# Twelve weight tiles held back instead of eight in the last block of an output product, and the last row tile's layer norm on VectorE alone

## The chip, the cores and the metric

The kernel runs on one core of a Trainium2 chip. Its metric is the device time of one execution in microseconds, the median of three runs. The engines spoken of here are TensorE (PE in the profile, its weight loads PEld), VectorE (DVE), ScalarE (ACT), GpSimd (POOL) and SyncE (SP), which issues most of the transfers between the chip's memory (HBM) and the on-chip memory SBUF. TensorE writes its sums into PSUM.

## What is computed

One layer of a decoder trunk on an input of 512 rows and 2048 columns, in float32. Three attention branches are gated, summed to y, multiplied by an output matrix of 2048 x 2048, added to the scaled input and normalised row by row:

```python
y = (jax.nn.sigmoid(p["gate_fox"]) * br_fox + jax.nn.sigmoid(p["gate_swa"]) * br_swa
     + jax.nn.sigmoid(p["gate_moba"]) * br_moba)
out = jnp.einsum('bsd,de->bse', y, w_out)
return layer_norm(DEEPNORM_ALPHA * x + out, ln_g, ln_b)

def layer_norm(x, g, b):
    xf = x.astype(jnp.float32)
    mu = jnp.mean(xf, axis=-1, keepdims=True)
    var = jnp.mean(jnp.square(xf - mu), axis=-1, keepdims=True)
    return ((xf - mu) * lax.rsqrt(var + LN_EPS) * g + b).astype(x.dtype)
```

The change touches only the last product and the norm.

## The kernel before

Every float32 operand of a matmul is split into a high part, rounded to TensorE's format, and a low part, the remainder; a product is then three matmuls (high x high, low x high, high x low). ScalarE makes the high part of a weight tile (L145), VectorE the low part (L148).

**The output product.** It is tiled into four column blocks `ec` of 512 columns, four row tiles `st` of 128 rows and sixteen k tiles of 128. The weights come as tiles of 128 x 512, two of them in one load of 512 KB; a load goes to one of four buffers `raw`, and it is issued by SyncE once both tiles of the load four places earlier have been split. `prepare(i + 2)` splits a tile two steps ahead of its use. In the first three column blocks a step uses one weight tile for all four row tiles, and after the sixteenth step `residual` (L944, L945) adds the scaled input to each row tile's sum and takes the statistics of that block with `bn_stats`.

**The last column block.** Its row tile 3 is computed in two halves of 256 columns with sums of their own, so that a step has nine matmuls of 512 columns and six of 256. The first eight weight tiles are used as they come. The last eight are split into tiles of their own, `wh0` to `wh7` and `wl0` to `wl7`, which stay in SBUF (`held`); their steps in `out_step` return at once. After the loop over all steps, the held tiles are used row tile by row tile: 24 matmuls finish row tile 0, 24 row tile 1, 24 row tile 2, then 24 each of half the width finish the two halves of row tile 3. Behind each of the row tiles 0 to 2 its `residual` and its `norm` are written; the residual of the first half of row tile 3 (`residual_half`, L1043 and L1044) stands in the middle of the norm of row tile 2, that of the second half and `norm(3)` stand at the end.

**The norm of a row tile.** VectorE combines the statistics (L971), ScalarE takes the square root (L972), VectorE the reciprocal (L983) and the shift -mean/deviation (L984, one column). The 2048 columns are then shared in pieces of 512. The columns below `cut` belong to VectorE: L976 subtracts the mean and multiplies by the gain, L979 multiplies by the reciprocal and adds the bias. In the columns from `cut` on, ScalarE normalises (L987) and GpSimd multiplies by the gain (L988) and adds the bias (L989). `cut` is 1024 for the row tiles 0 to 2 and 1536 for row tile 3. SyncE stores the pieces (L998, L1002, L1006, L1007).

**Memory.** `open_last` runs after the fourth step of the first column block. It opens the pool `last`, which holds the four row tiles `z0` to `z3` with the input (loaded by GpSimd's queue, L919), gain and bias (L923), and the held weight tiles. The pool `ozy`, which held the attention branches' outputs, stays open until the end of the kernel.

Each engine works through its instructions in the order in which they are written here; no scheduler moves them.

Of the kernel before, what the change touches and what calls it, by code (L numbers as in the profile page):

```python
# [9 lines left out]
F32R = mybir.dt.float32r  # L10
# [3 lines left out]
P = 128  # L14
S = 512
D = 2048
# [71 lines left out]
def hybrid_kernel(ctx: ExitStack, tc: tile.TileContext, a: dict, out: bass.AP):  # L88
    nc = tc.nc
# [19 lines left out]
    def acc_tile(name):  # L109
        return psum.tile([P, S], F32, tag="acc", name=name, bufs=3)  # L110
# [10 lines left out]
    raws, parts = {}, {}  # L121
    held = {}
    tasks = {}

    def at(i, order, f, *args):
        tasks.setdefault(i, []).append((order, len(tasks.get(i, ())), f, args))
# [369 lines left out]
            at((m - 56) // 2, 3, f, len(GROUPS) - 1, *args)  # L496


    att_ctx = ExitStack()
    ozy = work = const = vfox = vswa = sinkc = nsink = tri = causal = band = vld = None  # L500

    def open_attention():
        nonlocal ozy, work, const, vfox, vswa, sinkc, nsink, tri, causal, band, vld
        gate_ctx.close()
        ozy = ctx.enter_context(tc.tile_pool(name="ozy", bufs=12))
        work = att_ctx.enter_context(tc.tile_pool(name="work", bufs=2))
        const = att_ctx.enter_context(tc.tile_pool(name="const", bufs=1))
        const.tile([P, 32], F32, name="room")
        vfox = const.tile([P, 4, NH, P], F32R, tag="v", name="vfox")
        vswa = const.tile([P, 4, 2, P], F32R, name="vswa")  # L510
        sinkc = const.tile([P, NH], F32, name="sinkc")
        nsink = const.tile([P, NH], F32, name="nsink")
        vld = [work.tile([P, 4, NV], F32, tag="pth", name=f"vld{j}") for j in range(2)]
        for j in range(2):
            nc.sync.dma_start(vld[j], a["vs"][j])
        nc.gpsimd.dma_start(sinkc, a["sinks"].to_broadcast([P, NH]))
        ones = work.tile([P, S], F32, tag="L", name="ones", bufs=3)
        nc.gpsimd.memset(ones, 8.0)
        tri = work.tile([P, S], F32R, tag="L", name="tri", bufs=3)
        nc.gpsimd.affine_select(tri, ones, pattern=[[1, S]], compare_op=ALU.is_ge, fill=0.0, base=0,  # L520
                                channel_multiplier=-1)
        causal = const.tile([P, P], F32, name="causal")
        nc.gpsimd.memset(causal, 0.0)
        nc.gpsimd.affine_select(causal, causal, pattern=[[-1, P]], compare_op=ALU.is_ge, fill=8 * NEG, base=0,
                                channel_multiplier=1)
        band = const.tile([P, 256], F32, name="band")
        nc.gpsimd.iota(band, pattern=[[1, 256]], base=-P, channel_multiplier=-1,
                       allow_small_or_imprecise_dtypes=True)
        nc.gpsimd.affine_select(band, band, pattern=[[-1, 256]], compare_op=ALU.is_ge, fill=NEG, base=P,
                                channel_multiplier=1)  # L530
        nc.gpsimd.affine_select(band, band, pattern=[[1, 256]], compare_op=ALU.is_ge, fill=NEG, base=-1,
                                channel_multiplier=-1)
# [205 lines left out]
    where = {}  # L738
# [66 lines left out]
    for p in range(4):  # L805
        q, k, z = [], [], []
# [10 lines left out]
    for p in range(4):  # L817
        q, z = [], []
# [16 lines left out]
    for p in range(4):  # L835
        q, k, z = [], [], []
# [76 lines left out]

    def open_last():
        mix_ctx.close()
        last = box["last"] = ctx.enter_context(tc.tile_pool(name="last", bufs=1))
        for st in range(4):
            zr.append(last.tile([P, D], F32, name=f"z{st}"))
            nc.gpsimd.dma_start(zr[st], a["xn"][st])  # L919
            stats.append(last.tile([P, 5 if st == 3 else 4, 6], F32, name=f"stats{st}"))  # L920
        for n in ("ln_gain", "ln_bias"):
            box[n] = last.tile([P, D], F32, name=n)
            nc.gpsimd.dma_start(box[n], a[n].to_broadcast([P, D]))  # L923
        box["eps"] = last.tile([P, 1], F32, name="epst")
        nc.vector.memset(box["eps"], LN_EPS)
        for n in range(8):
            held[where["o", 3] + 8 + n] = tuple(last.tile([P, S], F32R, name=f"w{x}{n}") for x in "hl")

    oacc = {}

    def out_mm(st, k, hi, lo, half=None):

        sl = slice(st * P, (st + 1) * P)
        o = oacc[st]
        if half is not None:
            cs = slice(half * 256, (half + 1) * 256)
            o, hi, lo = oacc[3 + half][:, :256], hi[:, cs], lo[:, cs]
        nc.tensor.matmul(o, yb["h"][:, k, sl], hi, start=(k == 0), stop=False)  # L938
        nc.tensor.matmul(o, yb["l"][:, k, sl], hi, start=False, stop=False)  # L939
        nc.tensor.matmul(o, yb["h"][:, k, sl], lo, start=False, stop=(k == KD - 1))  # L940
# [6 lines left out]
    def out_step(i):  # L947
        _, ec, k = ids[i]
        if k == 0:
            for st in range(4):  # L950
                oacc[st] = (acc_tile if st == 3 else att_tile)("o")
            if ec == 3:
                oacc[4] = acc_tile("o")
        if ec == 3 and k >= 8:
            return
        hi, lo = parts.pop(i)
        for st in range(3 if ec == 3 else 4):
            out_mm(st, k, hi, lo)
        if ec == 3:
            out_mm(3, k, hi, lo, 0)  # L960
            out_mm(3, k, hi, lo, 1)
        if k == KD - 1:
            for st in range(4):
                at(i, 9, residual, ec, st, oacc[st])

    def norm(st, middle=None):

        last = st == 3
        cut = 1536 if last else 1024
        mv = box["last"].tile([P, 5], F32, tag="mv", name="mv", bufs=2)  # L970
        nc.vector.bn_aggr(mv[:, 0:2], stats[st].rearrange("p a b -> p (a b)"))  # L971
        nc.scalar.activation(mv[:, 2:3], mv[:, 1:2], AF.Sqrt, bias=box["eps"])  # L972
        g, b, z, rows = box["ln_gain"], box["ln_bias"], zr[st], out[st * P:(st + 1) * P]

        def first(cs):
            nc.vector.scalar_tensor_tensor(z[:, cs], z[:, cs], mv[:, 0:1], g[:, cs], op0=ALU.subtract, op1=ALU.mult)  # L976

        def second(cs):
            nc.vector.scalar_tensor_tensor(z[:, cs], z[:, cs], mv[:, 3:4], b[:, cs], op0=ALU.mult, op1=ALU.add)  # L979

        left = [slice(c, c + S) for c in range(0, cut, S)]
        first(left[0])
        nc.vector.reciprocal(mv[:, 3:4], mv[:, 2:3])  # L983
        nc.vector.scalar_tensor_tensor(mv[:, 4:5], mv[:, 0:1], -1.0, mv[:, 3:4], op0=ALU.mult, op1=ALU.mult)  # L984
        for c in range(cut, D, S):
            cs = slice(c, c + S)
            nc.scalar.activation(z[:, cs], z[:, cs], AF.Identity, bias=mv[:, 4:5], scale=mv[:, 3:4])  # L987
            nc.gpsimd.tensor_tensor(out=z[:, cs], in0=z[:, cs], in1=g[:, cs], op=ALU.mult)  # L988
            nc.gpsimd.tensor_tensor(out=z[:, cs], in0=z[:, cs], in1=b[:, cs], op=ALU.add)  # L989
        for cs in left[1:]:  # L990
            first(cs)
        if middle:
            second(left[0])
            middle()
            left = left[1:]
            for cs in left:
                second(cs)
            nc.sync.dma_start(rows[:, :cut], z[:, :cut])  # L998
        else:
            for cs in left[:2]:  # L1000
                second(cs)
            nc.sync.dma_start(rows[:, :2 * S], z[:, :2 * S])  # L1002
            for cs in left[2:]:
                second(cs)
        if last:
            nc.sync.dma_start(rows[:, 2 * S:cut], z[:, 2 * S:cut])  # L1006
        nc.sync.dma_start(rows[:, cut:], z[:, cut:])  # L1007


    at(2, 9, open_attention)  # L1010
    dests = ([("fox", 0, 5, 0)], [("fox", 5, 3, 0), ("swa", 0, 2, 192)])
    for st in range(4):
# [19 lines left out]
    for i in range(len(ids)):  # L1032
# [4 lines left out]
        step[ids[i][0]](i)  # L1037
        for _, _, f, args in sorted(tasks.pop(i, ()), key=lambda x: x[:2]):
            f(*args)
    first = where["o", 3] + 8  # L1040
    def residual_half(c):
        z = zr[3][:, 3 * S + c * 256:3 * S + (c + 1) * 256]
        nc.vector.scalar_tensor_tensor(z, z, ALPHA, oacc[3 + c][:, :256], op0=ALU.mult, op1=ALU.add)  # L1043
        nc.vector.bn_stats(stats[3][:, 3 + c], z)  # L1044

    for st in range(3):
        for n in range(8):
            out_mm(st, 8 + n, *parts[first + n])
        if st == 2:
            for c in range(2):  # L1050
                for n in range(8):
                    out_mm(3, 8 + n, *parts[first + n], c)
        residual(3, st, oacc[st])
        norm(st, (lambda: residual_half(0)) if st == 2 else None)
    residual_half(1)
# [68 lines left out]
```

## Time and profile before

| | |
|---|---|
| median of three runs | 1357.22 us (1357.11 to 1358.02) |
| the profiled execution | 1355.71 us |
| its span, first to last instruction | 1354.0 us |
| TensorE busy | 1325.5 us, 98% |
| VectorE busy | 910.1 us, 67% |
| ScalarE busy | 650.6 us, 48% |
| GpSimd busy | 192.0 us, 14% |
| moved by DMA | 174.43 MB, 129 GB/s in the mean |

Times in the rows are microseconds from the start of the span. Matmuls are pipelined: a matmul's own length overlaps the next one's, so the distance between two starts tells the pace. The busy time of GpSimd is rough.

### The profile page before, as it was taken

The numbers are of one execution on the slowest core, as the hardware profiler recorded it, in microseconds if no ns is written. First come the engines' busy times: TensorE is split into PE (matmuls) and PEld (weight loads), VectorE is DVE, ScalarE is ACT, GpSimd is POOL, SyncE is SP. The second block draws the span as 40 slices with busy tenths as digits, with TensorE's granted clock in tenths as the row PEclk, the third lists the DMA queues.
The fourth block names the chain that finished last, engine by engine and source line by source line (L and its number), as shares of the span: only waits on it lengthen the run. The fifth ranks groups of instructions, "written<-read, shape, count | busy, mean of one in ns | idle before, by whom it ended". The sixth has DMA issues, their size and how long they took to land.

```text
span 1354.0 us, 18416 instructions
## 1 busy us (share of the span) xinstructions
PE 1325.5 (98%) x6435; PEld 1116.1 (82%) x6435; DVE 910.1 (67%) x1627; ACT 650.6 (48%) x1190; POOL 192.0 (14%) x256
## 2 busy tenths in 40 slices
PE   8999999999999999999999999999999999999994
PEld 7978788888888887788889998888888888888884
DVE  6878878888888878566665656455547666533248
ACT  4544645455554646556565556556554222222231
POOL 5530000000000000121222332122220000000006
PEclk9999999999999999999999999999999999999997
DMA  7743517081533514432323222322226555542323
GB/s 233 223 148 131 188 42 282 11 281 45 215 112 121 198 32 133 158 94 84 109 70 98 63 96 65 94 78 79 78 79 200 180 183 184 204 169 93 94 78 124
DMA packets 57676, 174.43 MB, mean 129 GB/s; under 512 B 6552, under 2 KB 8088, under 8 KB 56816
## 3 DMA queue, kind: packets, MB, share of 16 engines
q1 hardware_dynamic: 46960, 147.44, 33.3%
q10 hardware_dynamic: 8064, 13.91, 2.7%
q0 software_dynamic: 2560, 11.90, 2.6%
q8 instruction: 50, 0.82, 0.2%
q14 instruction: 42, 0.34, 0.1%
HBM read 155.12 MB, written 18.12 MB: 128 GB/s over the span
## 4 chain that ended last, share of the span: by engine, by line
PE 93%; DVE 3%; DMA 2%; issue 1%; ACT 0%; SPq 0%; DVEq 0%; POOL 0%; ACTq 0%
PE br L879 10%; PE h L751 9%; PE h L753 9%; PE h L752 9%; PE beta L321 4%; PE beta L319 4%; PE beta L320 4%; PE o L938 4%; PE o L940 4%; PE o L939 4%; PE gamma L321 3%; PE gamma L319 3%; PE gamma L320 3%; PE alpha L321 3%; PE alpha L319 3%; PE alpha L320 3%
## 5 line engine op out<-in xcount | busy, mean ns | idle before, releaser
L145 ACT ACTIVATE hi<-raw 128x512 fp32r<-128x512 f32 x252 | 158.9, 631 | 333.1 <-PE o L939 106.1
L148 DVE TENSOR_TENSOR lo<-raw,hi 128x512 fp32r<-128x512 f32 x252 | 176.8, 706 | 159.4 <-ACT hi L145 134.9
L751 PE MATMUL h<-xh,hi 128*128 128x512 f32 x528 | 208.0, 394 | 0.0
L753 PE MATMUL h<-xh,lo 128*128 128x512 f32 x528 | 206.6, 391 | 0.0
L752 PE MATMUL h<-xl,hi 128*128 128x512 f32 x528 | 206.1, 390 | 0.0
L753 PEld LDWEIGHTS h<-xh,lo 128*128 128x128 f32 x528 | 99.1, 188 | 22.0 <-DVE lo L148 0.5
L752 PEld LDWEIGHTS h<-xl,hi 128*128 128x128 f32 x528 | 99.3, 188 | 18.6
L751 PEld LDWEIGHTS h<-xh,hi 128*128 128x128 f32 x528 | 99.2, 188 | 18.4
L667 POOL TENSOR_SCALAR lt<-lt,st 128x128 f32<-128x128 f32 (+2 forms) x96 | 70.8, 737 | 289.0 <-DVE st L666 287.2
L116 ACT ACTIVATE ghi<-rawd 128x512 fp32r<-128x512 f32 x96 | 60.7, 632 | 70.6 <-DVE glo L117 52.1
L116 ACT ACTIVATE ghi<-rawb 128x512 fp32r<-128x512 f32 x96 | 60.7, 632 | 69.9 <-DVE glo L117 48.0
L938 PE MATMUL o<-hi,yh 128*128 128x512 f32 (+1 forms) x232 | 88.8, 383 | 0.0
L939 PE MATMUL o<-hi,yl 128*128 128x512 f32 (+1 forms) x232 | 88.6, 382 | 0.0
L940 PE MATMUL o<-lo,yh 128*128 128x512 f32 (+1 forms) x232 | 88.6, 382 | 0.0
L116 ACT ACTIVATE ghi<-rawa 128x512 fp32r<-128x512 f32 x96 | 60.6, 633 | 58.0 <-PE alpha L320 22.2
L117 DVE TENSOR_TENSOR glo<-rawd,ghi 128x512 fp32r<-128x512 f32 x96 | 66.3, 691 | 27.2 <-ACT ghi L116 24.9
L117 DVE TENSOR_TENSOR glo<-rawb,ghi 128x512 fp32r<-128x512 f32 x96 | 66.2, 690 | 18.9 <-ACT ghi L116 17.7
L321 PE MATMUL alpha<-glo,xh 128*128 128x512 f32 x192 | 75.3, 392 | 1.6 <-DVE glo L117 1.4
L321 PE MATMUL beta<-glo,sh 128*128 128x512 f32 x192 | 74.8, 390 | 1.2 <-DVE glo L117 1.2
L879 PE MATMUL br<-hi,ozh 128*128 128x512 f32 x192 | 75.3, 392 | 0.0
L879 PE MATMUL br<-lo,ozh 128*128 128x512 f32 x192 | 74.9, 390 | 0.0
L319 PE MATMUL alpha<-ghi,xh 128*128 128x512 f32 x192 | 74.8, 390 | 0.0
(230 smaller groups left out, 3105.4 us busy)
## 6 DMA issues: line engine op xcount, KB each, us to landing
raw<-in_ws SPq DMA_DIRECT2D x130, 512.0 KB, 3.5
rawa<-in_wa SPq DMA_DIRECT2D x24, 512.0 KB, 4.4
rawc<-in_wa SPq DMA_DIRECT2D x24, 512.0 KB, 5.7
rawd<-in_wa SPq DMA_DIRECT2D x24, 512.0 KB, 5.7
sig<-gate_tiles SPq DMA_DIRECT2D x48, 256.0 KB, 3.8
rawb<-in_wa SPq DMA_DIRECT2D x20, 512.0 KB, 3.5
rawv<-in_wv SPq DMA_DIRECT2D x15, 324.0 KB, 3.4
xraw<-in_xT SPq DMA_DIRECT2D x16, 256.0 KB, 4.9
```

The lines of the kernel that those rows point to most:

```text
L116: nc.scalar.activation(hi, raw, AF.Copy)
L145: nc.scalar.activation(hi, raw, AF.Copy)
L148: nc.vector.tensor_sub(lo, raw, hi.bitcast(F32))
L319: nc.tensor.matmul(o, sth[:, us], hi, start=first, stop=False, skip_group_check=True)
L321: nc.tensor.matmul(o, sth[:, us], lo, start=False, stop=last, skip_group_check=True)
L751: nc.tensor.matmul(accs[t], hi[:, cc], xh[:, k], start=(k == 0), stop=False)
L752: nc.tensor.matmul(accs[t], hi[:, cc], xl[:, k], start=False, stop=False)
L753: nc.tensor.matmul(accs[t], lo[:, cc], xh[:, k], start=False, stop=(k == KD - 1))
L879: nc.tensor.matmul(bracc[g, st], o[:, 4 * b + kt, ss], w, start=(kt == 0 and n == 0), stop=(kt == 3 and n == 2))
L938: nc.tensor.matmul(o, yb["h"][:, k, sl], hi, start=(k == 0), stop=False)
L939: nc.tensor.matmul(o, yb["l"][:, k, sl], hi, start=False, stop=False)
L940: nc.tensor.matmul(o, yb["h"][:, k, sl], lo, start=False, stop=(k == KD - 1))
```

## The change

In the last column block four weight tiles are used as they come and twelve are held; a row tile then takes 36 matmuls where it took 24. The held tiles are allocated first in the pool `last`, and the pool `ozy` is closed before that pool is opened, so that `last` takes its room too. In `norm(3)` `cut` is 2048: VectorE does all four pieces, ScalarE's L987 and GpSimd's L988 and L989 have no piece of row tile 3, and the third and the fourth piece are stored as soon as each is done. Two lines are added further up, so most line numbers in the new kernel are one to three higher (L938 to L940 become L939 to L941, L976 and L979 become L977 and L980).

```diff
     def open_last():
         mix_ctx.close()
+        ozy_ctx.close()
         last = box["last"] = ctx.enter_context(tc.tile_pool(name="last", bufs=1))
+        for n in range(12):
+            held[where["o", 3] + 4 + n] = tuple(last.tile([P, S], F32R, name=f"w{x}{n}") for x in "hl")
...
-        for n in range(8):
-            held[where["o", 3] + 8 + n] = tuple(last.tile([P, S], F32R, name=f"w{x}{n}") for x in "hl")
...
-        if ec == 3 and k >= 8:
+        if ec == 3 and k >= 4:
             return
...
         last = st == 3
-        cut = 1536 if last else 1024
+        cut = D if last else 1024
...
             for cs in left[2:]:
                 second(cs)
-        if last:
-            nc.sync.dma_start(rows[:, 2 * S:cut], z[:, 2 * S:cut])
-        nc.sync.dma_start(rows[:, cut:], z[:, cut:])
+                if last:
+                    nc.sync.dma_start(rows[:, cs], z[:, cs])
+        if cut < D:
+            nc.sync.dma_start(rows[:, 2 * S:], z[:, 2 * S:])
...
-    first = where["o", 3] + 8
+    first = where["o", 3] + 4
...
     for st in range(3):
-        for n in range(8):
-            out_mm(st, 8 + n, *parts[first + n])
+        for n in range(12):
+            out_mm(st, 4 + n, *parts[first + n])
         if st == 2:
             for c in range(2):
-                for n in range(8):
-                    out_mm(3, 8 + n, *parts[first + n], c)
+                for n in range(12):
+                    out_mm(3, 4 + n, *parts[first + n], c)
```

TensorE's order where the streamed tiles end and the held ones begin, in the kernel before: the second half of row tile 3 (`o_11868`) with the eighth streamed tile (`hi_11967`), then row tile 0 (`o_11864`) with the first two held tiles, the ninth and tenth of the block.

```order
L938 MATMUL o_11868<-hi_11967,yh_10119 128x256
L939 MATMUL o_11868<-hi_11967,yl_10120 128x256
L940 MATMUL o_11868<-lo_11968,yh_10119 128x256
L938 MATMUL o_11864<-wh0_11065,yh_10119 128x512
L939 MATMUL o_11864<-wh0_11065,yl_10120 128x512
L940 MATMUL o_11864<-wl0_11066,yh_10119 128x512
L938 MATMUL o_11864<-wh1_11067,yh_10119 128x512
```

The same place in the new kernel, where `o_11877` is the second half of row tile 3, `hi_11896` the fourth streamed tile, and `o_11873` row tile 0:

```order
L939 MATMUL o_11877<-hi_11896,yh_10119 128x256
L940 MATMUL o_11877<-hi_11896,yl_10120 128x256
L941 MATMUL o_11877<-lo_11897,yh_10119 128x256
L939 MATMUL o_11873<-wh0_11048,yh_10119 128x512
L940 MATMUL o_11873<-wh0_11048,yl_10120 128x512
L941 MATMUL o_11873<-wl0_11049,yh_10119 128x512
L939 MATMUL o_11873<-wh1_11050,yh_10119 128x512
```

The switch now stands four weight tiles earlier, behind the fourth instead of the eighth; `wh0` is the fifth tile of the block.

VectorE's last instructions in the kernel before, from the residual of the second half of row tile 3 (`z_11056`) on:

```order
L1043 SCALAR_TENSOR_TENSOR z_11056<-z_11056,o 128x256
L1044 BN_STATS stats_11058<-z_11056 128x6
L971 BN_AGGR mv<-stats_11058 128x2
L976 SCALAR_TENSOR_TENSOR z_11056<-z_11056,mv,ln_gain 128x512
L983 RECIPROCAL mv<-mv 128x1
L984 SCALAR_TENSOR_TENSOR mv<-mv 128x1
L976 SCALAR_TENSOR_TENSOR z_11056<-z_11056,mv,ln_gain 128x512 x2
L979 SCALAR_TENSOR_TENSOR z_11056<-z_11056,mv,ln_bias 128x512 x3
```

The same in the new kernel, where row tile 3 is `z_11081`:

```order
L1045 SCALAR_TENSOR_TENSOR z_11081<-z_11081,o 128x256
L1046 BN_STATS stats_11083<-z_11081 128x6
L972 BN_AGGR mv<-stats_11083 128x2
L977 SCALAR_TENSOR_TENSOR z_11081<-z_11081,mv,ln_gain 128x512
L984 RECIPROCAL mv<-mv 128x1
L985 SCALAR_TENSOR_TENSOR mv<-mv 128x1
L977 SCALAR_TENSOR_TENSOR z_11081<-z_11081,mv,ln_gain 128x512 x3
L980 SCALAR_TENSOR_TENSOR z_11081<-z_11081,mv,ln_bias 128x512 x4
```

One instruction of each kind is added, for the last 512 columns; nothing else on VectorE has another place in this stretch.

## Rows read from the trace of the kernel before

**Rows 1.** The page: its span, and the chain that ended last, by engine.

```profile
span 1354.0 us, 18416 instructions
...
PE 93%; DVE 3%; DMA 2%; issue 1%; ACT 0%; SPq 0%; DVEq 0%; POOL 0%; ACTq 0%
```

**Rows 2.** Timeline of TensorE, last column block (start, length, engine, line, operation, out<-in).

```profile
1302.93 0.40 PE L938 MATMUL o<-hi,yh 128*128 128x512 f32 x1
...
1314.05 0.40 PE L938 MATMUL o<-wh,yh 128*128 128x512 f32 x1
...
1319.66 0.39 PE L938 MATMUL o<-wh,yh 128*128 128x512 f32 x1
...
1330.86 0.28 PE L938 MATMUL o<-wh,yh 128*128 128x256 f32 x1
...
1336.20 0.28 PE L940 MATMUL o<-wl,yh 128*128 128x256 f32 x1
```

**Rows 3.** Timeline of VectorE, row tile 0 and the start of row tile 1.

```profile
1319.86 0.69 DVE L944 SCALAR_TENSOR_TENSOR z<-z,o 128x512 f32<-128x512 f32 x1 [7.10 <-PE o L940]
...
1322.28 0.16 DVE L983 RECIPROCAL mv<-mv 128x1 f32<-128x1 f32 x1
...
1323.20 2.44 DVE L979 SCALAR_TENSOR_TENSOR z<-z,mv,ln_bias 128x512 f32<-128x512 f32 x2
1325.57 0.67 DVE L944 SCALAR_TENSOR_TENSOR z<-z,o 128x512 f32<-128x512 f32 x1
```

**Rows 4.** Timeline of VectorE, second half of row tile 3.

```profile
1339.82 0.41 DVE L1043 SCALAR_TENSOR_TENSOR z<-z,o 128x256 f32<-128x256 f32 x1
...
1341.05 1.74 DVE L976 SCALAR_TENSOR_TENSOR z<-z,mv,ln_gain 128x512 f32<-128x512 f32 x1
...
1342.89 1.03 DVE L984 SCALAR_TENSOR_TENSOR mv<-mv 128x1 f32<-128x1 f32 x1
```

**Rows 5.** The chain in order of time, its end (start, length, what).

```profile
1343.92 1.32 DVE z L976 x2
1345.24 1.67 DVE z L979
...
1348.58 0.66 DVE z L979
```

**Rows 6.** Timeline of GpSimd, row tiles 0, 2 and 3.

```profile
1323.56 1.54 POOL L988 TENSOR_TENSOR z<-z,ln_gain 128x512 f32<-128x512 f32 x1 [150.20 <-ACT z L987]
...
1328.12 1.62 POOL L989 TENSOR_TENSOR z<-z,ln_bias 128x512 f32<-128x512 f32 x1
...
1340.98 1.26 POOL L988 TENSOR_TENSOR z<-z,ln_gain 128x512 f32<-128x512 f32 x1
1342.31 1.59 POOL L989 TENSOR_TENSOR z<-z,ln_bias 128x512 f32<-128x512 f32 x1
...
1346.44 1.59 POOL L989 TENSOR_TENSOR z<-z,ln_bias 128x512 f32<-128x512 f32 x1
```

**Rows 7.** Timeline of SyncE, first and last store of row tile 3.

```profile
1348.61 0.33 SPq L1002 DMA_DIRECT2D out<-z  x1
...
1349.69 0.55 SPq L1007 DMA_DIRECT2D out<-z  x1
```

**Rows 8.** Timeline of SyncE, sixth weight load of the last block.

```profile
1296.95 0.33 SPq L131 DMA_DIRECT2D raw<-in_ws  x1
```

**Rows 9.** DMA issues from 1289 to 1312 (count, KB each, median us to landing).

```profile
raw<-in_ws SPq DMA_DIRECT2D x4, 512.0 KB, 3.6
```

**Rows 10.** Timeline of VectorE, low parts of weight tiles in the last block.

```profile
1295.64 1.28 DVE L148 TENSOR_TENSOR lo<-raw,hi 128x512 fp32r<-128x512 f32 x2
...
1307.07 3.70 DVE L148 TENSOR_TENSOR wl<-raw,wh 128x512 fp32r<-128x512 f32 x6
```

**Rows 11.** Line L919, the loads of the row tiles (least, median, most).

```profile
L919 POOL DMA_DIRECT2D z<-in_xn x4: 528/537/603, 1170.1 to 1171.8; - x4
...
DMA to landing us min/median/max: 6.5/11.1/15.1
```

More of the change, by code (lines that the diff above doesn't have):

```diff
@@ L496, in hybrid_kernel @@
             at((m - 56) // 2, 3, f, len(GROUPS) - 1, *args)
-    att_ctx = ExitStack()
+    att_ctx, ozy_ctx = ExitStack(), ExitStack()
     ozy = work = const = vfox = vswa = sinkc = nsink = tri = causal = band = vld = None
@@ L504, in open_attention @@
         gate_ctx.close()
-        ozy = ctx.enter_context(tc.tile_pool(name="ozy", bufs=12))
+        ozy = ozy_ctx.enter_context(tc.tile_pool(name="ozy", bufs=12))
         work = att_ctx.enter_context(tc.tile_pool(name="work", bufs=2))
```

## The prediction

> **What bounds the kernel now.** I read the chain of waits first, then the last 60 us engine by engine. Over the whole span the chain lies on TensorE for 93% [rows 1], so for most of the kernel nothing but fewer matmul cycles would help, and the change removes no matmul. The exception is the end. In the last column block TensorE works through its first eight weight tiles until 1314.05, then through the held ones row tile by row tile: row tile 0 from 1314.05 to 1319.66, row tiles 1 and 2 until 1330.86, the two halves of row tile 3 until its last matmul starts at 1336.20 [rows 2]. It has no gap there. The span is 1354.0, so 18 us pass after TensorE's last instruction. VectorE had been idle for 7.10 us when row tile 0 reached it at 1319.86 [rows 3]; from then on it is never idle. It finishes row tile 0 at 1325.57 [rows 3], gets to the last half of row tile 3 at 1339.82 [rows 4], 3.5 us after TensorE had it ready, and ends at 1349.24 [rows 5]. So TensorE sets the start of the tail, and a queue of four row tiles on VectorE sets its length. Each row tile costs VectorE more than the time between two deliveries: 24 matmuls of 0.2335 us ((1330.86 - 1314.05) / 72) are 5.60 us, row tile 0 takes 5.71 us, and the next two about 7.1 us each ((1339.82 - 1325.57) / 2).
>
> What stretches those two is GpSimd. The longest case is the last one: an instruction of L979 lasts 1.67 us, then 0.66 us when GpSimd is done (1346.44 + 1.59) [rows 5, 6]. At row tile 3, L976 starts at 1341.05 and takes 1.74 us; GpSimd's L988 runs from 1340.98 to 1342.24, and L976 ends 0.55 us after that. L984, on a single column, takes 1.03 us and ends at 1343.92, where GpSimd's L989 (1342.31 + 1.59) ends too [rows 4, 6]. The rows read as a wait for GpSimd's instruction to end, and it falls on VectorE instructions with two operands in SBUF; the residual of row tile 1 (L944, 0.67 us) ran beside L989 of row tile 0 at its usual length [rows 3].
>
> **The change, part by part.** (1) Twelve weight tiles are held instead of eight. TensorE's instructions are the same in number and size, so its end stays at 1336.20 plus the last matmul; only the order moves. Four streamed tiles end where the fifth began, at 1302.93 [rows 2]. Row tile 0 then needs 36 matmuls, 36 x 0.2335 = 8.41 us: its end moves from 1319.66 to 1311.34, those of row tiles 1 and 2 come at 1319.74 and 1328.15. VectorE follows 0.20 us behind (1319.86 against 1319.66), so it starts row tile 0 at 1311.54, 8.3 us earlier, and is done at 1317.25 by the 5.71 us of row tile 0. It waits for row tile 1 until 1319.94, is done at 1325.65, waits until 1328.35. Deliveries 8.41 us apart leave 2.7 us free after each, and GpSimd, which ends 9.88 us after VectorE's start (1328.12 + 1.62 against 1319.86) [rows 3, 6], overlaps the next row tile only for 1.5 us, beside its residual and statistics, which are not stretched. Row tile 2 reaches its second L979 form 4.0 us after its start, at 1332.35. The first half of row tile 3 is due at 1332.24 + 0.20, so it follows at once; with the remaining piece, one wait for GpSimd included, VectorE is free by about 1334.3. The second half is due 0.11 + 0.20 us after the last matmul's start, at 1336.51, and now VectorE waits for it. The residual of that half thus moves from 1339.82 to 1336.51: **-3.3 us**.
>
> (2) Row tile 2's GpSimd work. By the same 9.88 us it ends at 1328.35 + 9.88 = 1338.23. The first normalising instruction of row tile 3 is due 1.23 us after its residual (1339.82 to 1341.05), at 1337.74. It waits for GpSimd until 1338.23 and ends 0.55 us later, at 1338.78; undisturbed, 1338.40. So 0.4 us of the 1.08 us that the wait cost before (1.74 - 0.66) stays: **-0.7 us**. The tiny L984 finds GpSimd done: the pair of L983 and L984 took 0.26 us at row tile 0 (1322.28 to 1323.20 less one L976 of 0.66), against 1.13 us from 1342.79 to 1343.92 at row tile 3: **-0.9 us**.
>
> (3) The last column quarter of row tile 3 moves to VectorE. That adds two instructions of 0.66 us [rows 5], +1.32, and takes away the two waits that GpSimd's two instructions on this tile caused, 2 x (1.67 - 0.66) = -2.02: **-0.7 us**. ScalarE loses one instruction and GpSimd two, none of which ended last. In time: 1338.78 + 0.26 + 3 x 0.66 + 4 x 0.66 = 1343.66, against 1349.24: -5.6 us.
>
> The trace says that sharing this quarter with GpSimd cost more than it saved. [...]
>
> (4) The stores. Before, the first store of row tile 3 was issued at 1348.61, the last at 1349.69 [rows 7]; the span ends 5.39 us after the one and 4.31 us after the other. Now the first goes at 1342.36 and the last at 1343.68 with the same bytes: an end at 1347.75 or 1347.99. I take 1347.9, since either may bind. Measured from VectorE's last instruction (4.76 us) it would be 1348.4, the dear end.
>
> (5) Weight supply. Four more splits and two more loads come in a burst, since the steps from the fifth weight tile on issue no matmul. The splits are hidden: VectorE makes a low part every 0.61 us (3.70 / 6), starting at 1295.64 [rows 10], so the fifth tile's is done by 1298 and the sixteenth's, if its data are there, by 1304.3; TensorE wants them from 1302.93 on, one per three matmuls, 0.70 us. The loads have a buffer of four. The sixth load starts at 1296.95 as before [rows 8], the next two as soon as the fifth to eighth low parts are made, at about 1298.2 and 1299.4 instead of 1301.6 and 1307.2. One load lands 3.6 us after issue [rows 9]. Overlapped fully, the last lands at 1303.0; one after another, at 1296.95 + 3 x 3.6 = 1307.8. TensorE needs the fifteenth tile ten steps in, at 1309.9. Even the dear end leaves 0.8 us after a split of 0.6 on each of two engines, so: nothing. Below nothing there is no room, as TensorE has no gap to fill. Beyond that each us late costs a us.
>
> (6) The larger pool. It takes the room of the attention outputs as well, which shifts the addresses of the row tiles, gain and bias. Their loads were issued from 1170.1 and took up to 15.1 us [rows 11]; they are first used twelve weight tiles later, some 33 us by the 2.78 us per tile of rows 2. Some 17 us cover: nothing.
>
> Sum: -3.3 - 0.7 - 0.9 - 0.7 and -0.5 in the drain (4.76 to about 4.25) give **-6.1 us**: span 1347.9. The profiled execution took 1355.71, 1.7 us more than its span; the median is 1357.22, so 1357.22 - 6.1 = **1351.1 us**. Something under 2.7 us (0.2%) cannot be told from no change.
>
> **The rivals.** *GpSimd stays in the way.* If its work on row tile 2 runs on by more than half a us, L976 and L984 of row tile 3 pay their old waits, 1.08 and 0.95 instead of 0.4 and 0: +1.65, 1352.7. For it: the estimate leaves GpSimd only 0.5 us inside row tile 3. Against: VectorE is idle from 1334.3 to 1336.5, which can only help GpSimd.
>
> *The loads starve TensorE; this is the one that ends slower.* Its place is the fifteenth weight tile of row tile 0, the point from which it decides a last load landing after about 1308.6, its price one us per us, since TensorE's end then moves and everything follows. A landing at 1311 gives 1353.5; to be slower than before it must be later than 1314.7, three loads in 18 us where one takes 3.6. Against it: the bound of fully serial loads.
>
> *The change does not free VectorE.* If row tile 0 doesn't get to VectorE early, because something in the held path orders the matmuls behind all the splits, the queue stays and only part (3) is left: 1356.5. Against it: the first held matmul needs only its own weight tile.
>
> **How the numbers follow.** Forecast 0.78, GpSimd rival 0.10, starvation 0.08 (of it 0.02 slower, 0.01 same, the rest faster), change without effect 0.04 (same). So faster 0.93, same 0.05, slower 0.02. The forecast's own bounds are 1350.6 (no wait on GpSimd, the cheap drain) and 1351.6 (the dear drain); the three runs of before lie 0.9 us apart, and the GpSimd rival must be held: 1349.9 to 1353.2.
>
> **What would show it.** Right: TensorE's first held matmul near 1302.9 and its last still near 1336.2 without idle time; VectorE idle some 2.5 us before the residuals of row tiles 1 and 2 and about 2 us before the last half; seven instructions of 0.66 us at the end, with no 1.67 among them; a drain of 4.3 us. Wrong: idle time on TensorE released by a load or a split after 1302.9; a first normalising instruction of row tile 3 over 1.5 us; VectorE without idle time before row tile 3.

## The result, and the profile after

The new kernel takes 1350.24 us (median of six runs, 1346.17 to 1351.06) against 1357.49 us of the kernel before beside it; the ratio is 0.9942, 95% interval [0.9931, 0.9954]. That is the ratio of the means of the six runs (1349.78 over 1357.70); the medians give 0.9947. It is faster, by more than the bound of 0.2%. The forecast was 1351.1 us. The profiled execution took 1350.06 us, with a span of 1348.4 us, 5.6 us shorter than before [rows 1]. The median of 1350.24 lies inside the range of 1349.9 to 1353.2; the ratio applied to the 1357.22 us of before gives 1349.35 us, which is 0.55 us below the range.

The page of the new kernel, its span and the chain that ended last:

```profile
span 1348.4 us, 18408 instructions
...
PE 94%; DMA 2%; DVE 2%; issue 1%; ACT 1%; SPq 0%; DVEq 0%; POOL 0%; ACTq 0%
```

VectorE's share of the chain fell from 3 to 2%. TensorE's timeline (start, length, engine, line, operation), at the first held matmul of row tiles 0, 1 and 2, the first of row tile 3, and the last of all:

```profile
1304.03 0.40 PE L939 MATMUL o<-wh,yh 128*128 128x512 f32 x1
...
1312.22 0.39 PE L939 MATMUL o<-wh,yh 128*128 128x512 f32 x1
...
1320.38 0.39 PE L939 MATMUL o<-wh,yh 128*128 128x512 f32 x1
...
1328.54 0.28 PE L939 MATMUL o<-wh,yh 128*128 128x256 f32 x1
...
1337.05 0.28 PE L941 MATMUL o<-wl,yh 128*128 128x256 f32 x1
```

The last block began 1.10 us later in this execution than in the one of before. TensorE's timelines, before and now, at the block's first matmul of 256 columns:

```profile
1293.88 0.28 PE L938 MATMUL o<-hi,yh 128*128 128x256 f32 x1
```

```profile
1294.98 0.28 PE L939 MATMUL o<-hi,yh 128*128 128x256 f32 x1
```

From there on I count times from that matmul, since it is the same work in both kernels; "the block's length" below is the time from it to the end of the span: 60.13 us before, **53.38 us** now, 6.75 less. (For these lengths I take the spans to the thousandth that the trace keeps, 1354.011 and 1348.361; the page rounds them to a tenth.) The last matmul starts 42.07 us into the block (42.32 before [rows 2]). VectorE's timeline (in brackets the idle time before, and what ended it), from the residual of row tile 0 to the last instruction:

```profile
1312.42 0.69 DVE L945 SCALAR_TENSOR_TENSOR z<-z,o 128x512 f32<-128x512 f32 x1 [5.15 <-PE o L941]
...
1320.58 0.69 DVE L945 SCALAR_TENSOR_TENSOR z<-z,o 128x512 f32<-128x512 f32 x1 [2.36 <-PE o L941]
...
1328.74 0.69 DVE L945 SCALAR_TENSOR_TENSOR z<-z,o 128x512 f32<-128x512 f32 x1 [2.37 <-PE o L941]
...
1337.37 0.42 DVE L1045 SCALAR_TENSOR_TENSOR z<-z,o 128x256 f32<-128x256 f32 x1 [2.78 <-PE o L941]
...
1338.61 0.75 DVE L977 SCALAR_TENSOR_TENSOR z<-z,mv,ln_gain 128x512 f32<-128x512 f32 x1
...
1339.47 0.16 DVE L985 SCALAR_TENSOR_TENSOR mv<-mv 128x1 f32<-128x1 f32 x1
1339.55 2.07 DVE L977 SCALAR_TENSOR_TENSOR z<-z,mv,ln_gain 128x512 f32<-128x512 f32 x3
1341.54 2.73 DVE L980 SCALAR_TENSOR_TENSOR z<-z,mv,ln_bias 128x512 f32<-128x512 f32 x4
```

The queue of [rows 3, 4] is gone. VectorE now waits for TensorE before every row tile, and before the last half too, where it was 3.5 us late before. The first normalising instruction of row tile 3 takes 0.75 us instead of 1.74, the one on a single column 0.16 instead of 1.03, and none of the last seven is stretched. GpSimd's last instruction is over before that:

```profile
1337.07 1.26 POOL L990 TENSOR_TENSOR z<-z,ln_bias 128x512 f32<-128x512 f32 x1
```

It ends at 1338.33, 0.28 us before VectorE's L977 at 1338.61. SyncE's stores of row tile 3:

```profile
1342.97 0.33 SPq L1003 DMA_DIRECT2D out<-z  x1
1343.63 0.99 SPq L1007 DMA_DIRECT2D out<-z  x2
```

VectorE ends at 1344.27, the span 4.09 us later (4.76 before); this time is called the drain below. TensorE never waits in the block. The burst of loads held up ScalarE, whose high parts waited for the last two loads, and VectorE's low parts behind it, by 0.64 and 1.19 us:

```profile
1301.59 1.15 ACT L145 ACTIVATE wh<-raw 128x512 fp32r<-128x512 f32 x2 [2.06 <-DMA raw<-in_ws]
1304.08 2.38 ACT L145 ACTIVATE wh<-raw 128x512 fp32r<-128x512 f32 x4 [1.33 <-DMA raw<-in_ws]
```

### The profile page after: what moved, and what is told of

It reads as the page before. It is cut to its first block, busy times and chain, and to the rows that moved or that the text cites. A ratio compares the mean times of both kernels' runs of the same rounds, so it can differ in the third digit from the quotient of the medians.

```text
span 1348.4 us, 18408 instructions
## 1 busy us (share of the span) xinstructions
PE 1326.3 (98%) x6435; PEld 1116.7 (83%) x6435; DVE 903.6 (67%) x1629; ACT 649.8 (48%) x1189; POOL 188.1 (14%) x254
## 4 chain that ended last, share of the span: by engine, by line
PE 94%; DMA 2%; DVE 2%; issue 1%; ACT 1%; SPq 0%; DVEq 0%; POOL 0%; ACTq 0%
PE br L879 10%; PE h L751 9%; PE h L753 9%; PE h L752 9%; PE beta L321 4%; PE beta L320 4%; PE beta L319 4%; PE o L941 4%; PE o L940 4%; PE o L939 4%; PE gamma L321 3%; PE alpha L321 3%; PE gamma L319 3%; PE gamma L320 3%; PE alpha L320 3%; PE alpha L319 3%
## 5 line engine op out<-in xcount | busy, mean ns | idle before, releaser
L148 DVE TENSOR_TENSOR lo<-raw,hi 128x512 fp32r<-128x512 f32 x248 | 174.1, 706 | 151.9 <-ACT hi L145 127.4
L939 PE MATMUL o<-hi,yh 128*128 128x512 f32 (+1 forms) x212 | 81.8, 386 | 0.0
L940 PE MATMUL o<-hi,yl 128*128 128x512 f32 (+1 forms) x212 | 81.7, 385 | 0.0
L941 PE MATMUL o<-lo,yh 128*128 128x512 f32 (+1 forms) x212 | 81.7, 385 | 0.0
```

The source lines that it names most:

```text
L148: nc.vector.tensor_sub(lo, raw, hi.bitcast(F32))
```

## The experiments

Ratios are to the kernel before, run beside each. The other columns come from the profiled executions, in us from the block's first matmul of 256 columns.

| kernel | ratio, 95% interval | last residual | VectorE ends | drain | block's length |
|---|---|---|---|---|---|
| before | | 45.94 | 55.37 | 4.76 | 60.13 |
| before, again | 0.9995 [0.9987, 1.0004] | 45.94 | 55.36 | 4.77 | 60.13 |
| new | 0.9942 [0.9931, 0.9954] | 42.39 | 49.29 | 4.09 | 53.38 |
| new, again | 0.9947 [0.9933, 0.9960] | 42.38 | 49.28 | 4.09 | 53.37 |
| twelve held, norm shared | 0.9953 [0.9940, 0.9966] | 42.39 | 49.98 | 4.77 | 54.75 |
| eight held, norm on VectorE | 0.9988 [0.9979, 0.9996] | 45.93 | 54.67 | 4.10 | 58.77 |
| ten held | 0.9955 [0.9940, 0.9971] | 42.43 | 50.91 | 4.11 | 55.02 |
| sixteen held | 0.9972 [0.9962, 0.9983] | 45.77 | 52.67 | 4.10 | 56.77 |
| new layout, order of before | 1.0002 [0.9992, 1.0011] | 45.81 | 55.25 | 4.75 | 60.00 |
| new, held tiles placed last | 0.9955 [0.9938, 0.9972] | 42.63 | 49.53 | 4.10 | 53.63 |
| gain and bias in PSUM | 0.9943 [0.9930, 0.9955] | 42.39 | 47.94 | 4.78 | 52.72 |
| uneven halves, four stores | 0.9961 [0.9948, 0.9973] | 44.71 | 51.34 | 3.51 | 54.85 |
| four stores | 0.9957 [0.9944, 0.9970] | 42.39 | 49.30 | 3.50 | 52.80 |
| PSUM and four stores | 0.9947 [0.9934, 0.9959] | 42.39 | 47.94 | 4.17 | 52.11 |

**Both kernels once more.** What repeats, and how far?

> The kernel before, submitted as if it were a change: the ratio to itself should be 1.000 within 0.001, and the first matmul of its last column block should start within about 1 us of 1291.84. How far both are off tells what a difference of one profile, and of one comparison, is worth.

> The changed kernel once more, to see how much of its gain comes from the last column block. Theory of the tail: from the first matmul of the last column block to the end of the span it takes 55.4 us against 62.2 us before, 6.7 us less; everything ahead of that block is unchanged, so the time should be 6.7 us under the kernel before, about 1350.7 against 1357.4, ratio 0.9951 (0.9945 to 0.9957). Rival, something ahead of the last block got faster too (the pools lie elsewhere): ratio 0.9942 or below again, and the first matmul of the last block starts before 1291.8 us in the trace.

Block lengths repeat within 0.01 us, but the block's start does not: 1293.88 us in the first profile of before, 1295.89 in the second, 1294.98 and 1295.30 in the new kernel, 1296.10 at the latest (four stores). The scatter arises in the first 490 us. The last matmul of line 319 that adds to `alpha` starts at 488.2 in the first profile of before and at 490.4 in the second, and what follows, to the last transposition of line 908, takes 681.1 and 680.9 us. From that transposition to the block's first narrow matmul, the stretch in which `open_last` stands, both kernels take 124.6 us (1169.3 to 1293.88 before, 1170.4 to 1294.98 now). So what the change touches ahead of the block costs and gains nothing. What delayed the second profile is not shown. Two of TensorE's waits in the first 490 us, first before, then before again (total, times, longest):

```profile
PE va L245 <- ACT xh L116: 4.5, 1, 4.5
PE alpha L321 <- DVE glo L117: 1.4, 2, 1.0
```

```profile
PE alpha L321 <- DVE glo L117: 2.9, 4, 1.8
PE va L245 <- ACT xh L116: 1.9, 2, 1.5
```

One is 1.5 us longer in the second profile, the other 2.6 us shorter, and the five waits that the view lists there add up to 8.9 and 8.8 us. So one pair of totals does not settle 1 us, while the block's length tells 0.1 us. The change's own gain is 6.75 us, a ratio of 1 - 6.75 / 1357.2 = 0.9950, inside both intervals.

**Twelve held, the norm shared as before** (against the new kernel):

```diff
-        cut = D if last else 1024
+        cut = 1536 if last else 1024
...
-                if last:
-                    nc.sync.dma_start(rows[:, cs], z[:, cs])
-        if cut < D:
-            nc.sync.dma_start(rows[:, 2 * S:], z[:, 2 * S:])
+        if last:
+            nc.sync.dma_start(rows[:, 2 * S:cut], z[:, 2 * S:cut])
+        nc.sync.dma_start(rows[:, cut:], z[:, cut:])
```

> Twelve tiles held, but row tile 3's last 512 columns still go through ScalarE and GpSimd. Theory (the end of TensorE sets the start of the tail, and GpSimd makes VectorE wait in it): the last half residual starts as early as in the changed kernel, but two instructions of L979's kind take about 1.67 us each again and two of 0.66 us are saved, so VectorE ends 0.7 us later than in the changed kernel: about 1351.4, ratio 0.9956. Rival (sharing the quarter with GpSimd relieves VectorE): 1.3 us faster than the changed kernel, 1349.4.

The holding alone brings 5.39 us. The waits on row tile 2's GpSimd work are gone here too, but GpSimd's own two instructions on row tile 3 stretch VectorE's L980. Timelines of VectorE and of GpSimd:

```profile
1339.86 4.08 DVE L980 SCALAR_TENSOR_TENSOR z<-z,mv,ln_bias 128x512 f32<-128x512 f32 x3
```

```profile
1339.54 1.52 POOL L989 TENSOR_TENSOR z<-z,ln_gain 128x512 f32<-128x512 f32 x1 [2.23 <-ACT z L988]
1341.13 1.59 POOL L990 TENSOR_TENSOR z<-z,ln_bias 128x512 f32<-128x512 f32 x1
```

Three L980 in 4.08 us here, four in 2.73 us in the new kernel. VectorE ends 0.69 us later although it has two instructions less, and the drain, which the expectation left out, stays at 4.77. The rival, that sharing relieves VectorE, falls for operands in SBUF.

**Eight held, the norm on VectorE alone** (against the kernel before; the stores as in the new kernel):

```diff
-        cut = 1536 if last else 1024
+        cut = D if last else 1024
```

> Eight tiles held as before, only row tile 3's norm is VectorE's alone. Theory: VectorE's queue of row tiles 0 to 2 stays as it was, so the last half residual starts near 1339.8 us as before, and only the two waits on GpSimd against two more instructions remain: 0.7 us less, 1356.7, ratio 0.9995. Rival (the queue at the end is relieved mostly by this part): 3 us less or more.

VectorE ends 0.70 us earlier, as part (3) had it, and the drain, which the expectation left out, is 0.66 us shorter; 1.36 together. The waits on row tile 2's GpSimd work stay, since the queue stays:

```profile
1343.18 1.74 DVE L976 SCALAR_TENSOR_TENSOR z<-z,mv,ln_gain 128x512 f32<-128x512 f32 x1
...
1345.02 1.03 DVE L984 SCALAR_TENSOR_TENSOR mv<-mv 128x1 f32<-128x1 f32 x1
```

5.39 + 1.36 = 6.75, as for both together: the parts add up.

**Ten and sixteen held** (for ten; sixteen likewise with 16 and 0):

```diff
-        if ec == 3 and k >= 4:
+        if ec == 3 and k >= 6:
...
-        for n in range(12):
-            out_mm(st, 4 + n, *parts[first + n])
+        for n in range(10):
+            out_mm(st, 6 + n, *parts[first + n])
```

> The changed kernel with ten tiles held instead of twelve. From the first matmul of 256 columns in the last block to the end of the span, the kernel before takes 60.1 us, norm_only (eight held) 58.8, the changed kernel 53.4. Theory (once a row tile's matmuls take longer than VectorE's 5.7 us for it, the end of TensorE sets the tail and more held tiles bring nothing): 30 matmuls take 7.0 us, so VectorE is on time for the last half; only GpSimd's work on row tile 2 now reaches into row tile 3 and makes its first normalising instruction wait about 1.1 us: 54.5 us, ratio 0.9959. Rival (each held tile brings its share): half of the way from eight to twelve, 56.1 us, ratio 0.9970.

> All sixteen tiles of the last block held, to see the starvation rival at work. Theory: TensorE catches up with the supply; the third tile's low part stands on VectorE behind the residuals of the third block (stall about 2.6 us) and the seventh load lands about 1 us late, and each us of stall moves the end of TensorE and of the kernel by a us: 53.4 + 3.6 = 57.0 us from the first matmul of the block, ratio 0.9977. Rival (loads and splits keep up, VectorE gets more slack): as fast as the changed kernel or faster, ratio 0.9950.

At ten tiles the rival "GpSimd stays in the way" is there to be seen. VectorE, then GpSimd:

```profile
1338.78 1.46 DVE L977 SCALAR_TENSOR_TENSOR z<-z,mv,ln_gain 128x512 f32<-128x512 f32 x1
...
1340.34 1.03 DVE L985 SCALAR_TENSOR_TENSOR mv<-mv 128x1 f32<-128x1 f32 x1
```

```profile
1339.76 1.59 POOL L990 TENSOR_TENSOR z<-z,ln_bias 128x512 f32<-128x512 f32 x1
```

The residual is in time (42.43), but GpSimd runs until 1341.35, and both VectorE instructions are stretched beside it; VectorE ends 1.62 us later than with twelve. The expectation counted only the first of the two. At sixteen the other rival comes true. What TensorE waited for (total, times, longest), the two rows of the last block:

```profile
PE o L941 <- DVE wl L148: 2.2, 1, 2.2
...
PE o L939 <- ACT wh L145: 0.3, 1, 0.3
```

No matmul is left to cover the splits. TensorE waits for 2.5 us, and its last matmul starts 3.4 us later than with twelve (45.45 against 42.07), since around the waits matmuls also follow one another at 0.34 to 0.39 us instead of 0.23. The block takes 56.8 us. (In this kernel the matmuls of 256 columns come last, so I count from 2.04 us after the block's first matmul at 1293.55; elsewhere nine matmuls of 512 columns fill this time ahead of the first narrow one.) Twelve lies between the two costs; fourteen was not run.

**The layout alone, and the layout undone.** The first has the order of before in the new memory layout, with room for twelve pairs of tiles; the second is the new kernel with the loop that allocates the held tiles moved to the end of `open_last`, where it stood before:

```diff
-        for n in range(12):
-            held[where["o", 3] + 4 + n] = tuple(last.tile([P, S], F32R, name=f"w{x}{n}") for x in "hl")
         for st in range(4):
...
         nc.vector.memset(box["eps"], LN_EPS)
+        for n in range(12):
+            held[where["o", 3] + 4 + n] = tuple(last.tile([P, S], F32R, name=f"w{x}{n}") for x in "hl")
```

> The kernel before in its order (eight tiles held, the last quarter of row tile 3 shared with GpSimd), but with the changed kernel's memory layout: the larger pool is opened in the place of two, and room for twelve held tiles is taken first, of which eight are used. Theory: the layout is worth nothing, the order does all. The stretch from the first 256-column matmul of the last block to the end of the span takes 60.1 us as before, the ratio is 1.000, and the held 512-column matmuls start 0.2335 us apart. Rival: the other addresses of weights or row tiles give TensorE the quicker pace that the changed kernel shows. Then the held matmuls start 0.227 us apart, row tile 2 is delivered about 0.5 us earlier, and the stretch takes 59.5 to 59.9 us.

> The changed kernel with one edit in the memory layout: the twelve held weight tiles are allocated last in the pool, behind row tiles, statistics, gain and bias, as in the kernel before, instead of first; the larger room stays, and every instruction keeps its place. Theory: the quicker pace of the held 512-column matmuls (0.2269 us from start to start against 0.2335) comes from the place of the held tiles, since the run with the new layout and the old order showed it too. Then the held matmuls start 0.2335 us apart again (0.1136 us at 256 columns), row tile 2 is delivered 0.71 us later, the last matmul 0.25 us later, the first normalising instruction of row tile 3 waits for GpSimd by 0.1 to 0.2 us, and the stretch from the first 256-column matmul of the block to the end of the span takes 53.7 to 53.9 instead of 53.4 us, a ratio near 0.9955. Rival: it is not the held tiles' place in the pool but the closing of the other pool, which moves all of it. Then the pace stays at 0.2269 us, and the stretch at 53.4 us.

TensorE in the first (72 matmuls of 512 columns from the first row to the second, then 48 of 256), and in the second (108, then 72):

```profile
1316.04 0.40 PE L941 MATMUL o<-wh,yh 128*128 128x512 f32 x1
...
1332.38 0.28 PE L941 MATMUL o<-wh,yh 128*128 128x256 f32 x1
...
1338.02 0.28 PE L943 MATMUL o<-wl,yh 128*128 128x256 f32 x1
```

```profile
1303.06 0.40 PE L939 MATMUL o<-wh,yh 128*128 128x512 f32 x1
...
1328.27 0.28 PE L939 MATMUL o<-wh,yh 128*128 128x256 f32 x1
...
1336.33 0.28 PE L941 MATMUL o<-wl,yh 128*128 128x256 f32 x1
```

(1332.38 - 1316.04) / 72 = 0.2269 us with the held tiles first in the pool, whatever the order of the work; (1328.27 - 1303.06) / 108 = 0.2334 with them last, whichever pools are closed. At 256 columns it is the other way round, 0.120 against 0.1135. The granted clock is 1.00, the higher of its two levels, in all these stretches, and y, the other operand, lies in a pool that the edit does not touch. So the place of the held tiles sets the pace, and the rival in the second run, the closing of the other pool, falls. In the order of before the quicker pace is worth 0.13 us of the block, since VectorE's queue ends last there; in the new order 0.25 us.

The second run also tells about the wait on GpSimd. VectorE, and GpSimd's last instruction:

```profile
1337.88 0.75 DVE L977 SCALAR_TENSOR_TENSOR z<-z,mv,ln_gain 128x512 f32<-128x512 f32 x1
```

```profile
1336.73 1.26 POOL L990 TENSOR_TENSOR z<-z,ln_bias 128x512 f32<-128x512 f32 x1
```

Row tile 2 comes as late here as the prediction had it, GpSimd ends at 1337.99, 0.11 us after L977 has started, and L977 still takes 0.75 us. I had expected a wait of 0.1 to 0.2 us; there is none. By the 0.55 us that the prediction counts from GpSimd's end, L977 would end at 1338.54, before its 1338.63, so an overlap as short as this need not show.

**Gain and bias of row tile 3 in PSUM**, with the last 512 columns back on ScalarE and GpSimd (against the new kernel). ScalarE copies the pieces:

```diff
+    def into_psum(what, c, make):
+        t = inps[what, c] = make("inps")
+        nc.scalar.activation(t, box["ln_gain" if what == "g" else "ln_bias"][:, c * S:(c + 1) * S], AF.Copy)
...
-        cut = D if last else 1024
+        cut = 1536 if last else 1024
...
+            bias = inps["b", cs.start // S] if last else b[:, cs]
-            nc.vector.scalar_tensor_tensor(z[:, cs], z[:, cs], mv[:, 3:4], b[:, cs], op0=ALU.mult, op1=ALU.add)
+            nc.vector.scalar_tensor_tensor(z[:, cs], z[:, cs], mv[:, 3:4], bias, op0=ALU.mult, op1=ALU.add)
```

> Twelve held; for row tile 3 gain and bias of the first 1536 columns are copied by ScalarE to free PSUM banks ahead of time, so VectorE's normalising instructions have one operand in SBUF; the last 512 columns go through ScalarE and GpSimd again, as in hold_only. Theory (VectorE waits for GpSimd only with two SBUF operands): the instructions beside GpSimd take 0.67 us, not 1.67 as in hold_only; VectorE ends 1.3 us earlier than in the changed kernel, GpSimd about 3.6 us behind the tiny L985, so the whole is 1.1 us less: 52.3 us, ratio 0.9943. Rival (GpSimd slows VectorE whatever the operands): the 1.67 us stay and it is no faster than hold_only, 54.7 us, ratio 0.9960.

VectorE's last five pieces, and GpSimd beside them:

```profile
1338.75 1.40 DVE L984 SCALAR_TENSOR_TENSOR z<-z,mv,inps 128x512 f32<-128x512 f32 x2
1340.06 2.06 DVE L988 SCALAR_TENSOR_TENSOR z<-z,mv,inps 128x512 f32<-128x512 f32 x3
```

```profile
1339.76 1.26 POOL L997 TENSOR_TENSOR z<-z,ln_gain 128x512 f32<-128x512 f32 x1 [2.22 <-ACT z L996]
1341.10 1.27 POOL L998 TENSOR_TENSOR z<-z,ln_bias 128x512 f32<-128x512 f32 x1
```

Three instructions in 2.06 us beside GpSimd, where three took 4.08 with the bias in SBUF; GpSimd itself is quicker, 1.26 instead of 1.52 to 1.59 us. So it is the second operand in SBUF that makes the two engines wait for each other. The Trainium skill, "SBUF — State Buffer", section "Who interferes with whom", states it so: a VectorE instruction with two inputs in SBUF contends with a GpSimd instruction that reads SBUF, one with at most one such input, outside its 2-port modes, doesn't. The trace agrees: 4.08 us with the bias in SBUF, 2.06 with it in PSUM.

Of the 1.35 us that VectorE gains, 0.69 go to the drain, which is 4.78 us again. Two stores fall due at about VectorE's end, and SyncE issues the second 0.42 us after the first:

```profile
1342.15 0.33 SPq L1015 DMA_DIRECT2D out<-z  x1
1342.57 0.55 SPq L1017 DMA_DIRECT2D out<-z  x1
```

It is so in the other kernels of the table with a drain of 4.75 to 4.77 us as well; in the new kernel the last store is issued at VectorE's end.

**The stores.** The first run splits row tile 3 into 384 and 128 columns instead of twice 256, and stores each 512 columns as soon as they are done, by SyncE and ScalarE in turn; the second changes only the stores of the new kernel; the third does that in the kernel with PSUM. The edit that they share:

```diff
-            for cs in left[:2]:
-                second(cs)
-            nc.sync.dma_start(rows[:, :2 * S], z[:, :2 * S])
-            for cs in left[2:]:
+            for cs in left:
                 second(cs)
                 if last:
-                    nc.sync.dma_start(rows[:, cs], z[:, cs])
+                    (nc.scalar if cs.start % 1024 else nc.sync).dma_start(rows[:, cs], z[:, cs])
```

> The changed kernel with row tile 3's last sum of 128 columns behind one of 384, instead of two of 256, and a store for each 512 columns of row tile 3, issued by SyncE and ScalarE in turn. Theory (the end of TensorE and what follows it set the time): the last residual and its statistics are 0.3 us shorter, the drain starts 0.66 us earlier and its end goes by the last store, 0.3 us less: 52.8 us, ratio 0.9947 or 0.0004 under the changed kernel's. Rival (matmuls of 128 columns cost as much as those of 256): TensorE ends 1 to 2 us later and the gain is lost, 54 us or more.

> The changed kernel with one more edit: row tile 3 is stored in four pieces of 512 columns, each as soon as it is done, issued by SyncE and ScalarE in turn, where the changed kernel stores 1024, 512 and 512 columns, all by SyncE. Theory: the time behind VectorE's last instruction (4.13 us in the changed kernel, 4.75 before) is set by the bytes that still have to go and by one queue issuing them one after another. Then it falls to about 3.5 us, as in the run with the uneven halves, VectorE's last instruction stays where it was (49.3 us behind the first 256-column matmul of the block), the stretch from that matmul to the end of the span takes 52.8 instead of 53.4 us, and the ratio to the kernel before is about 0.9946. Rival: the fixed cost of the last store alone sets that time, and the 3.5 us of the other run came from its different spacing. Then the stretch stays at 53.4 us and the ratio at 0.995.

> Gain and bias of row tile 3 lie in PSUM, GpSimd does the last 512 columns as in the kernel before, twelve tiles are held, and row tile 3 is stored in four pieces of 512 columns by SyncE and ScalarE in turn, the last behind GpSimd. Theory: with one operand in PSUM VectorE does not wait for GpSimd, so the quarter can be shared after all; what ate that gain was the long drain behind GpSimd's last instruction (4.78 us). With the smaller stores VectorE ends 47.9 us behind the first 256-column matmul of the block, GpSimd within 0.5 us of that, 3.5 to 3.9 us later the span ends: 51.4 to 52.3 us against 53.4 in the changed kernel and 60.1 before, a ratio of about 0.9938. Rival: the last store starts only when GpSimd has ended and its 4.1 us are fixed. Then the stretch takes 52.3 to 52.7 us, no better than with gain and bias in PSUM alone.

The smaller last piece lost: the end of TensorE's work came 2.3 us later. The matmuls of 384 columns are dearer than those of 256, 0.174 us against 0.120, and those of 128 columns hardly cheaper. Two rows of its timeline in succession:

```profile
1337.03 0.28 PE L941 MATMUL o<-wh,yl 128*128 128x128 f32 x1
1337.14 0.28 PE L942 MATMUL o<-wl,yh 128*128 128x128 f32 x1
```

They are 0.11 us apart, and so are the weight loads that go with them, one per matmul. The stores gained: 3.51 and 3.50 us from VectorE's end to the span's end, against 4.09 with three stores on one queue. Whether the second queue or the smaller first store did it was not separated, and the ratio of the four stores, 0.9957, does not show these 0.6 us. In the third run GpSimd ends at 1341.36 + 1.27 = 1342.63, 0.25 us after VectorE, and ScalarE issues the last store then. GpSimd's and ScalarE's timelines:

```profile
1341.36 1.27 POOL L998 TENSOR_TENSOR z<-z,ln_bias 128x512 f32<-128x512 f32 x1
```

```profile
1342.65 0.34 ACTq L1016 DMA_DIRECT2D out<-z  x1
```

The block takes 52.11 us, the shortest of all: 1.27 us less than the new kernel, inside what was expected, and below the 52.3 that the rival allowed at best. By its total (1348.55 us, ratio 0.9947) it cannot be told from the new kernel.

## Why the prediction was right or wrong

The mechanism of the tail was right: the queue on VectorE goes, and TensorE's end and VectorE's work behind it set the time. What failed are sizes, in three terms of the sum and in the range. The block got 6.75 us shorter where 6.1 were forecast. The block's clock, forecast against measured:

| | forecast | new kernel | held tiles placed last |
|---|---|---|---|
| residual of the last half | 42.63 | 42.39 | 42.63 |
| VectorE's end | 49.78 | 49.29 | 49.53 |
| drain | 4.25 | 4.09 | 4.10 |
| block's length | 54.0 | 53.38 | 53.63 |

- **(1) The queue goes.** VectorE waits 2.36, 2.37 and 2.78 us where 2.7, 2.7 and about 2 were forecast. The residual moved by 3.55 us instead of 3.3; the 0.24 is the pace of the held matmuls, since with the tiles in their old place the residual comes at 42.63, to the hundredth.
- **(2) Row tile 2's GpSimd work.** Mis-sized: I kept 0.4 us of the wait, and none was left. GpSimd's last instruction took 1.26 us, not the 1.62 of row tile 0 in [rows 6]; VectorE, idle before it, runs nothing with two operands in SBUF beside it now. In the run with the tiles placed last GpSimd ends 9.52 us after the residual of row tile 2, not 9.88. I wrote that the idle time "can only help GpSimd" and didn't put it into the sum. Of these 0.38 us (1338.78 less 1338.40) 0.25 show at VectorE's end, since the other steps behind the residual take 0.13 us more than forecast. The tiny L984 cost nothing, as forecast.
- **(3) The last quarter on VectorE.** -0.70 us, as forecast, by the run with eight tiles. That sharing costs more than it saves is shown both ways: put back in the new kernel, VectorE ends 0.69 us later.
- **(4) The stores.** -0.67 us where -0.5 was forecast. The first store's bound held: 5.39 us from its issue at 1342.97 to the end, 5.40 before.
- **(5) The loads.** Nothing, as forecast, and close to the cheap end. The last load released ScalarE at 1304.08, that is 1302.98 by the clock of before, where 1303.0 to 1307.8 were the bounds. The rival needs sixteen tiles to come true.
- **(6) The larger pool.** "Nothing" was wrong. I looked at when its loads land, not at where the held tiles lie. Their new place was worth 0.25 us, which is what (1) lacks.

So (1), (2) and (4) lack 0.24, 0.25 and 0.16, which is the 0.65. That alone gives 1357.22 - 6.75 = 1350.5 us, 0.1 below the forecast's own bounds and inside the range. The ratio's 1349.35 us lies outside, and the step that failed there is the one that sized the range: it took the 0.9 us between three runs of before for the scatter of a comparison, but the block's start alone moves by 2.2 us from execution to execution, upstream of anything that the change touches, and the ratio's own interval is 0.0012, or 1.6 us, to either side. That the ratio fell just below the range was chance in part. One of the six runs of the new kernel, at 1346.17 us, lies 3.8 us below the next; without it the means give 0.9947, as the medians and the second comparison do, and 1350.0 us, inside the range. No trace of that run was kept, so why it was fast stays open.

## What to carry to other kernels

When a late engine's queue sets the end, give it its work earlier at the price of order alone, and stop where the feeding engine starts to starve or the last piece comes too late; here twelve of sixteen tiles. Before sharing a tail between VectorE and GpSimd, look whether VectorE's instructions have two operands in SBUF: here the sharing then cost VectorE 0.7 us, and with one of the two operands in PSUM it saved 1.35 us. Where a change is confined to one stage, measure that stage's length in the trace: here it repeated within 0.01 us, while totals scattered by more than the terms in question.

## What was not expected of the hardware

The pace of the matmuls depends on where the moving operand lies in SBUF: 0.2269 against 0.2334 us at 512 columns, 0.120 against 0.1135 at 256, with nothing changed but the order of allocation in one pool and the granted clock at 1.00 in both. Which property of the address decides was not tried. A matmul of 128 columns with a weight load of its own is hardly quicker than one of 256, 0.11 us from start to start. And GpSimd's instruction on 128 x 512 elements takes 1.26 to 1.31 us where VectorE rests or has an operand in PSUM, and from 1.26 up to 1.68 us (row tile 2 of the new kernel) beside VectorE's instructions with two operands in SBUF.
